# Gates and late output projections of a decoder trunk: seven products of quarters for pairs of output tiles, on half of the K tiles

## Chip, core and metric

The program runs on one core of one Trainium2 chip. The metric is the device time of one execution in microseconds, as the median of the runs shown. All matrices are float32 in DRAM.

## The reference, cut to what matters

Two layers over 512 tokens of 2048 channels; layer 0 has a state-space (SSD) mixer, layer 1 a stick-breaking attention. After each mixer comes a gate with a small embedding:

```python
h = x
for i in range(2):
    u = rms_norm(h, norm_w[i])
    mix = ssd_branch(u, ...) if i == 0 else sb_branch(u, ...)   # ends in y @ out_w, 4096 or 2048 -> 2048
    h = h + mix
    gate = sigmoid(rms_norm(h, ple_norm_w[i]) @ ple_gate_w[i])  # 2048 -> 2048
    h = h + (p[i] @ ple_proj_w[i]) * gate                       # 256 -> 2048
```

## The kernel before

Channels lie on the 128 partitions, tokens (T = 512) along the free axis; a K tile is 128 input channels. Float32 products are made from split operands: each operand is a rounded part (`ah`, `wh`, type float32r) and the difference to it (`al`, `wl`), and `mm3` makes three matmuls of 128x128 by 128x512 per K tile: wh with ah, wh with al, wl with ah. ACT makes the rounded part, DVE the difference.

`unit` (L174) makes one tile of 128 output channels: for every 8 K tiles `block` (L130) loads 512 KB of weights into `raw` (2 buffers, issued by SP), ACT copies them to `wh`, DVE subtracts to `wl` (3 buffers each), at a raised priority so that they run ahead; then 24 matmuls accumulate in one bank of PSUM. Pools `mmp` and `pxp` hold four banks each. `Flow` chains all instructions of TensorE in the order in which they are traced, whatever the scheduler does on the other engines; those run in an order that a scheduler fixes at compile time, and SP's queue of DMA issues is one of them, in order too.

The stages that the change touches, in order: the second half of K of the SSD output projection (`w_out[j][:, KT:, :]`, L551 to L555, 16 units of 16 K tiles, operands loaded back from `y_d` by `staged` through four buffers `stg`); `ple(0)` (L513), the gate, 16 units of 16 K tiles with 6 more matmuls (`px_p`) each, operands split from `h` by `norm_acts`; the attention; 8 units of 8 K tiles of its output projection (L736) beside the last head; the rest of that projection (L745): 8 units with the second 8 K tiles, 8 with all 16; and `ple(1)`. The residual `h` stays in SBUF in 16 tiles from L493 on. `act_tiles` gives 16 pairs of operand tiles that all stages share, so operands of a new stage can be split only when the last unit of the old one has read that K tile. A pool opened for a stage lies where the previous stage's pool lay, and waits tile by tile for the last reader.

## Time and profile before

| | us |
|---|---|
| median of 3 runs | 2760.46 (2760.33 to 2760.82) |
| span of the profiled execution, first to last instruction | 2757.8 |
| median less span | 2.7 |
| PE busy | 2732.7 (99%) |
| DVE busy | 1597.3 (58%) |
| ACT busy | 1188.0 (43%) |
| POOL busy | 358.4 (13%) |
| granted clock of PE, mean | 1.000 |

The span is that of one profiled execution. PE is TensorE's matmuls, PEld its weight loads, which overlap with matmuls; busy time of PE contains the latency of a matmul, so its pace is read from the distance between starts.

### The profile page before, as it was taken

Reading aid. Unit: us, or ns where it says so; the run is one execution under the profiler, and the core shown is the slowest. Engines: PE = TensorE matmul, PEld = TensorE weight load, DVE = VectorE, ACT = ScalarE, POOL = GpSimd, SP = SyncE. Lnnn points to the kernel's source line nnn. Section 1 sums busy time; section 2 is a strip of 40 time slices with the busy share of each in tenths; the row PEclk is TensorE's granted clock in tenths of the full one; section 3 lists DMA queues with packets and bytes.
Section 4 is the critical chain, followed back from the end, with each engine's and each line's share of the span. In section 5 each row is a group of like instructions: output and inputs, shape, how many; then the busy total and the mean of one; then the engine's idle time right before and its main releaser. Section 6 shows DMA issues by size and latency. Waiting matters only on the chain.

```text
span 2757.8 us, 32622 instructions
## 1 busy us (share of the span) xinstructions
PE 2732.7 (99%) x12684; PEld 2247.4 (81%) x12684; DVE 1597.3 (58%) x2226; ACT 1188.0 (43%) x1700; POOL 358.4 (13%) x363
## 2 busy tenths in 40 slices
PE   8999999999999999999999999999999999999999
PEld 6888888888888878888888888888888888888887
DVE  8676766676676774243443547647647647743533
ACT  5443444444353442232333436546646546533321
POOL 2222221212222120001101100000000000011000
PEclk9999999999999999999999999999999999999999
DMA  4342323233332446343323322322222222332332
GB/s 160 109 130 92 130 92 126 93 118 106 116 123 97 141 137 202 119 139 98 96 95 100 96 96 85 100 96 84 87 90 92 81 95 89 110 126 100 107 116 91
DMA packets 98348, 300.53 MB, mean 109 GB/s; under 512 B 10960, under 2 KB 11088, under 8 KB 98192
## 3 DMA queue, kind: packets, MB, share of 16 engines
q1 hardware_dynamic: 98192, 298.44, 33.2%
q8 instruction: 99, 1.62, 0.2%
q14 instruction: 57, 0.47, 0.1%
HBM read 280.18 MB, written 18.22 MB: 108 GB/s over the span
## 4 chain that ended last, share of the span: by engine, by line
PE 89%; DVE 5%; ACT 2%; POOL 2%; DMA 1%; issue 1%; SPq 0%; ACTq 0%; POOLq 0%; DVEq 0%
PE mm L54 74%; PE pv L54 6%; PE px_p L54 2%; DVE wl L137 1%; DVE M L410 1%; PE px_r L54 1%; PE px_z L54 1%; PE px_av L54 1%; POOL y L437 1%; PE px_st L54 1%; ACT wh L135 1%; PE px_y L54 1%; DMA stg<-y_d 1%; DVE cv L339 1%; PE px_qn L54 1%
## 5 line engine op out<-in xcount | busy, mean ns | idle before, releaser
L54 PE MATMUL mm<-ah,wh 128*128 128x512 f32 x3312 | 1300.1, 393 | 1.0 <-ACT ah L142 1.0
L54 PE MATMUL mm<-ah,wl 128*128 128x512 f32 x3312 | 1291.7, 390 | 0.0
L54 PE MATMUL mm<-al,wh 128*128 128x512 f32 x3312 | 1290.1, 390 | 1.5 <-DVE al L143 1.3
L137 DVE TENSOR_TENSOR wl<-raw,wh 128x1024 fp32r<-128x1024 f32 x457 | 569.9, 1247 | 492.3 <-ACT wh L135 491.2
L135 ACT CAST wh<-raw 128x1024 fp32r<-128x1024 f32 x457 | 478.7, 1048 | 856.7 <-PE mm L54 729.2
L54 PEld LDWEIGHTS mm<-ah,wl 128*128 128x128 f32 x3312 | 621.6, 188 | 131.9
L54 PEld LDWEIGHTS mm<-al,wh 128*128 128x128 f32 x3312 | 622.1, 188 | 130.9 <-DVE al L143 3.9
L54 PEld LDWEIGHTS mm<-ah,wh 128*128 128x128 f32 x3312 | 622.0, 188 | 126.3 <-ACT ah L142 1.2
L503 POOL TENSOR_TENSOR ssq<-ssq,sq 128x512 f32<-128x512 f32 x45 | 71.8, 1596 | 620.0 <-ACT sq L502 620.0
L410 DVE TENSOR_SCALAR M<-ab,act__370 128x128 f32<-128x128 f32 x256 | 104.8, 452 | 41.1 <-PE px_y L54 27.9
L339 DVE SCALAR_TENSOR_TENSOR cv<-xr,vec,cv 128x512 f32<-128x512 f32 x144 | 108.7, 755 | 7.0 <-ACT cv L337 4.4
L650 POOL TENSOR_SCALAR_AFFINE_SELECT lm<-lm 128x128 f32<-128x128 f32 x64 | 28.0, 438 | 615.3 <-DVE lm L649 609.6
L54 PE MATMUL pv<-wh,ah 128*128 128x512 f32 x256 | 101.0, 395 | 0.3 <-DVE gt L532 0.3
L54 PE MATMUL pv<-wl,ah 128*128 128x512 f32 x256 | 99.9, 390 | 0.0
L54 PE MATMUL pv<-wh,al 128*128 128x512 f32 x256 | 99.7, 389 | 0.0
L532 DVE TENSOR_TENSOR gt<-mm,rbc 128x512 f32<-128x512 f32 x32 | 22.1, 691 | 103.6 <-PE mm L54 103.6
L205 POOL TENSOR_TENSOR xc<-cv,sg 128x512 f32<-128x512 f32 x32 | 42.6, 1331 | 262.0 <-ACT sg L204 262.0
L203 ACT ACTIVATE sg<-cv 128x512 f32<-128x512 f32 x48 | 30.4, 633 | 104.6 <-DVE cv L339 104.3
L647 DVE SCALAR_TENSOR_TENSOR lb<-px_z,e 128x128 f32<-128x128 f32 (+1 forms) x64 | 31.4, 490 | 72.7 <-ACT e L645 72.2
L417 ACT ACTIVATE eA<-ab 64x384 f32<-64x384 f32 x64 | 33.6, 525 | 62.8 <-POOL y L437 60.3
L205 POOL TENSOR_TENSOR zs<-zs,sg 128x512 f32<-128x512 f32 x32 | 41.6, 1300 | 139.0 <-ACT sg L204 128.6
L337 ACT ACTIVATE cv<-xr,vec 128x512 f32<-128x512 f32 x48 | 39.0, 812 | 45.2 <-DVE xr L335 45.2
(219 smaller groups left out, 2557.9 us busy)
## 6 DMA issues: line engine op xcount, KB each, us to landing
raw<-in_w_in SPq DMA_DIRECT2D x160, 512.0 KB, 3.6
raw<-in_w_sb SPq DMA_DIRECT2D x96, 512.0 KB, 3.6
raw<-in_w_out SPq DMA_DIRECT2D x64, 512.0 KB, 3.9
raw<-in_w_gate SPq DMA_DIRECT2D x64, 512.0 KB, 3.5
ab<-ac_d SPq DMA_DIRECT2D x64, 256.0 KB, 3.2
raw<-in_w_v SPq DMA_DIRECT2D x32, 512.0 KB, 3.6
raw<-in_w_sbo SPq DMA_DIRECT2D x32, 512.0 KB, 3.5
y_d<-zs SPq DMA_DIRECT2D x32, 256.0 KB, 4.3
```

Of the source, the lines that this page charges most:

```text
L54: self._queue(self.tc.nc.tensor.matmul(out, lhsT, rhs, start=start, stop=stop), rows / 2370.0)
L135: S.copy(wh, raw)
L137: V.tensor_tensor(wl, raw, wh.bitcast(F32), op=ALU.subtract)
L203: S.activation(tmp, half, AF.Tanh)
L205: G.tensor_tensor(dst, half, tmp, op=ALU.mult)
L337: S.activation(cv, xr[:, 3 : T + 3], AF.Identity, bias=cb[:, u : u + 1], scale=cw[:, u, 3:4])
L339: V.scalar_tensor_tensor(cv, xr[:, tap : tap + T], cw[:, u, tap : tap + 1], cv, op0=ALU.mult, op1=ALU.add)
L410: V.tensor_scalar(M[:, c, :], ab[:, c * P : (c + 1) * P], act_[:, c, h : h + 1], act_[:, c, h : h + 1], op0=ALU.min, op1=ALU.subtract,)
L417: S.activation(eA[pp, :], ab[pp, P:], AF.Exp)
L503: G.tensor_tensor(ssq, ssq, sq, op=ALU.add)
L647: V.scalar_tensor_tensor(lb, pz, 0.0, e, op0=ALU.min, op1=ALU.subtract)
L650: G.affine_select(out=lm[:, :P], in_=lm[:, :P], compare_op=ALU.is_gt, fill=0.0, base=0, pattern=[[1, P]], channel_multiplier=-1,)
```

## The change

In the four GEMMs named above two tiles of output channels are made together by `pair`. For half of the K tiles (`SP` = 4 couples of them; in the last projection the second 8 K tiles) the product of 2x2 quarters (two output tiles by two K tiles, two halves of 256 tokens) is made with seven products in place of eight, in Winograd's form: sums and differences of weight quarters (`wforms`: S1 to S4), sums and differences of operand quarters (`xforms`, once a stage), seven accumulations of 128x128 by 128x256 into four banks Z, W, X, Y, each again by three matmuls, and a few adds of the results (`E`). The other K tiles (`rest`) follow as before, accumulated into X and Y. The first four pairs of the last projection have no rest. `EARLY`, the number of first units of the SSD projection made beside the last scan, goes from 5 to 6; `raw` becomes 8 KB a partition, and the scratch of the software DMA queue is cut to 1024 bytes. The weights are laid out in DRAM accordingly.

```diff
...
-EARLY = 5
+EARLY = 6
+SP = 4
 EARLY_SB = 8
...
-            raw = wp.tile([P, 8, P], F32, tag="raw", name="raw", bufs=2)
+            raw = wp.tile([P, 16, P], F32, tag="raw", name="raw", bufs=2)[:, :8, :]
...
+    def wforms(src):
+        with tc.high_priority(offset=4000):
+            F = wp.tile([P, 8, 2, P], F32, tag="raw", name="raw", bufs=2)
+            nc.sync.dma_start(F.rearrange("p (a b) g m -> p a b (g m)", b=2)[:, :, 0, :], src)
+            V.tensor_tensor(F[:, 1], F[:, 0], F[:, 2], op=ALU.subtract)
+            V.tensor_tensor(
+                F[:, 2:6].rearrange("p (a b) g m -> p a b (g m)", b=2)[:, :, 1, :],
+                F[:, 4].rearrange("p g m -> p (g m)").unsqueeze(1).broadcast_to([P, 2, 2 * P]),
+                F[:, 0:2].rearrange("p a g m -> p a (g m)"),
+                op=ALU.add,
+            )
+            V.tensor_tensor(F[:, 7], F[:, 6], F[:, 5], op=ALU.subtract)
+            out = []
+            for tag, a, b, pool in (("", 1, 5, wp), ("3", 5, 8, wq)):
+                wh = pool.tile([P, 2 * (b - a), P], F32R, tag="wh" + tag, name="wh")
+                wl = pool.tile([P, 2 * (b - a), P], F32R, tag="wl" + tag, name="wl")
+                raw = F[:, a:b].rearrange("p a g m -> p (a g) m")
+                S.copy(wh, raw)
+                V.tensor_tensor(wl, raw, wh.bitcast(F32), op=ALU.subtract)
+                out += [(wh, wl, 2 * i) for i in range(b - a)]
+        return out
+    def xforms(raw, i, acts):
+        for q in range(2):
+            split(*acts[2 * i + q], raw[:, 2 * q : 2 * q + 2].rearrange("p a t -> p (a t)"))
+        V.tensor_tensor(
+            raw[:, 4:6], raw[:, 0:1].broadcast_to([P, 2, H]), raw[:, 1:3], op=ALU.subtract
+        )
+        V.tensor_tensor(raw[:, 6], raw[:, 2], raw[:, 4], op=ALU.subtract)
+        V.tensor_tensor(raw[:, 7], raw[:, 3], raw[:, 6], op=ALU.subtract)
+        th = tp.tile([P, 4, H], F32R, tag=f"th{i}", name=f"th{i}")
+        tl = tp.tile([P, 4, H], F32R, tag=f"tl{i}", name=f"tl{i}")
+        split(th, tl, raw[:, 4:8])
+        return th, tl
+    def pair(src, acts, forms, k0, rest, emit, xy=None):
+        xy = xy or (mmp, "mm")
+        Z, W = (mmp.tile([P, 2, H], F32, tag="mm", name="mm") for _ in range(2))
+        X, Y = (xy[0].tile([P, 2, H], F32, tag=xy[1], name="mm") for _ in range(2))
+        begun = set()
+        def seven(bank, half, w, g, xh, xl):
+            wh, wl, i = w
+            for a, b in ((wh, xh), (wh, xl), (wl, xh)):
+                fl.mm(bank[:, half], a[:, i + g, :], b, start=bank.name not in begun, stop=False, skip_group_check=True)
+                begun.add(bank.name)
+        for b in range(len(forms) // 2):
+            S3, A11, S1, A22, S2, A12, S4 = wforms(src[:, b, :].rearrange("p (a n) -> p a n", a=4))
+            for n in range(7):
+                for g in range(2):
+                    i = 2 * b + g
+                    (ah, al), (bh, bl) = acts[k0 + 2 * i], acts[k0 + 2 * i + 1]
+                    th, tl = forms[i]
+                    lo, hi = slice(0, H), slice(H, T)
+                    seven(*(
+                        (Z, 1, A11, g, ah[:, hi], al[:, hi]),
+                        (W, 1, S3, g, th[:, 1], tl[:, 1]),
+                        (W, 0, S1, g, th[:, 0], tl[:, 0]),
+                        (Z, 0, S2, g, th[:, 2], tl[:, 2]),
+                        (X, 1, A12, g, bh[:, hi], bl[:, hi]),
+                        (X, 0, S4, g, bh[:, lo], bl[:, lo]),
+                        (Y, 1, A22, g, th[:, 3], tl[:, 3]),
+                    )[n])
+                fl.poll()
+        E = tp.tile([P, 4, H], F32, tag="E", name="E")
+        S.copy(E[:, 1], Z[:, 1])
+        U2 = tp.tile([P, H], F32, tag="U2", name="U2")
+        V.tensor_tensor(U2, Z[:, 0], E[:, 1], op=ALU.add)
+        V.tensor_tensor(E[:, 0:4:3], W, U2.unsqueeze(1).broadcast_to([P, 2, H]), op=ALU.add)
+        V.tensor_tensor(E[:, 2], W[:, 0], E[:, 3], op=ALU.add)
+        for o, ps in ((0, X), (1, Y)):
+            flat = ps.rearrange("p a t -> p (a t)")
+            for b in range(len(rest) // 8):
+                wh, wl = block(src[:, len(forms) // 2 + o + b, :].rearrange("p (k n) -> p k n", n=P))
+                for k in range(8):
+                    xh, xl = acts[rest[8 * b + k]]
+                    for a, x in ((wh, xh), (wh, xl), (wl, xh)):
+                        fl.mm(flat, a[:, k, :], x, start=False, stop=False, skip_group_check=True)
+                    fl.poll()
+            a = 2 if rest or o == 0 else 1
+            V.tensor_tensor(E[:, 2 * o + 2 - a : 2 * o + 2], ps[:, 2 - a : 2], E[:, 2 * o + 2 - a : 2 * o + 2], op=ALU.add)
+            emit(o, E[:, 2 * o : 2 * o + 2].rearrange("p a t -> p (a t)"))
...
-    def norm_acts(w):
+    def norm_acts(w, k0=0):
         acts = []
-        for k in range(KT):
+        for k in range(k0, KT):
...
+    def raw_forms():
+        return tp.tile([P, 8, H], F32, tag="U", name="U")
+    def staged_forms(src, k0, k1):
+        acts, forms = [act_tiles(k % KT) for k in range(k0, k1)], []
+        for i in range((k1 - k0) // 2):
+            U = raw_forms()
+            for q in range(2):
+                k = k0 + 2 * i + q
+                nc.sync.dma_start(U[:, 2 * q : 2 * q + 2].rearrange("p a t -> p (a t)"), src[k * P : (k + 1) * P, :])
+            forms.append(xforms(U, i, acts))
+        return acts, forms
+    def add_h(ssq=None, lq=None, j0=0):
+        def emit(o, e):
+            j = j0 + o
+            V.tensor_tensor(h[j], h[j], e, op=ALU.add)
+            if ssq is not None:
+                add_sq(lq, ssq, j)
+        return emit
     def ple(lq, layer, ssq):
-        """h += (p W) sigmoid(norm(h) Wg), by tiles of 128 channels."""
-        acts = norm_acts(plw[layer])
+        w = plw[layer]
+        acts, forms = [act_tiles(k) for k in range(2 * SP)], []
+        for i in range(SP):
+            U = raw_forms()
+            for q in range(2):
+                k = 2 * i + q
+                S.activation(
+                    U[:, 2 * q : 2 * q + 2].rearrange("p a t -> p (a t)"), h[k], AF.Copy, scale=w[:, k : k + 1]
+                )
+            forms.append(xforms(U, i, acts))
+        acts += norm_acts(w, 2 * SP)
         rbc = start_row_scale(ssq)
-        pr = lq.tile([P, 2, T], F32, tag="pr", name="pr")
-        nc.sync.dma_start(pr, pT[layer].rearrange("(k p) t -> p k t", p=P))
         ph = lq.tile([P, 2, T], F32R, tag="ph", name="ph")
         pl = lq.tile([P, 2, T], F32R, tag="pl", name="pl")
-        split(ph, pl, pr)
+        for k in range(2):
+            pr = lq.tile([P, T], F32, tag="sq2", name="pr", bufs=2)
+            nc.sync.dma_start(pr, pT[layer][k * P : (k + 1) * P, :])
+            split(ph[:, k, :], pl[:, k, :], pr)
         nssq = rp.tile([P, T], F32, tag="ssq", name="ssq")
-        for j in range(KT):
-            if j % 4 == 0:
-                vh, vl = block(w_ple[layer, j // 4])
-            psp = px("px_p")
-            for k in range(2):
-                kk = 2 * (j % 4) + k
-                mm3(psp, vh[:, kk, :], vl[:, kk, :], ph[:, k, :], pl[:, k, :], k == 0, k == 1)
-            ps = unit(w_gate[layer, j], acts)
-            gt = lq.tile([P, T], F32, tag="gt", name="gt", bufs=2)
-            V.tensor_tensor(gt, ps, rbc, op=ALU.mult)
-            S.activation(gt, gt, AF.Sigmoid)
-            V.tensor_tensor(gt, psp, gt, op=ALU.mult)
-            V.tensor_tensor(h[j], h[j], gt, op=ALU.add)
-            if layer == 0:
-                add_sq(lq, nssq, j)
-            else:
-                nc.sync.dma_start(out[j * P : (j + 1) * P, :], h[j])
+        for jj in range(KT // 2):
+            psps = []
+            for o in range(2):
+                j = 2 * jj + o
+                if j % 4 == 0:
+                    vh, vl = block(w_ple[layer, j // 4])
+                psp = px("px_p")
+                for k in range(2):
+                    kk = 2 * (j % 4) + k
+                    mm3(psp, vh[:, kk, :], vl[:, kk, :], ph[:, k, :], pl[:, k, :], k == 0, k == 1)
+                psps.append(psp)
+            def emit(o, e):
+                j = 2 * jj + o
+                V.tensor_tensor(e, e, rbc, op=ALU.mult)
+                S.activation(e, e, AF.Sigmoid)
+                V.tensor_tensor(e, psps[o], e, op=ALU.mult)
+                V.tensor_tensor(h[j], h[j], e, op=ALU.add)
+                if layer == 0:
+                    add_sq(lq, nssq, j)
+                else:
+                    nc.sync.dma_start(out[j * P : (j + 1) * P, :], h[j])
+            pair(w_gate[layer, jj], acts, forms, 0, range(2 * SP, KT), emit)
         return nssq
 
     with ExitStack() as st:
+        wq = st.enter_context(tc.tile_pool(name="wq0", bufs=2, reuse_waits="tile"))
+        tp = st.enter_context(tc.tile_pool(name="tp0", bufs=1, reuse_waits="tile"))
         lq = st.enter_context(tc.tile_pool(name="lq0", bufs=1, reuse_waits="tile"))
         for j in range(KT):
             h.append(lp.tile([P, T], F32, tag=f"h{j}", name=f"h{j}"))
             nc.sync.dma_start(h[j], (h_d if j < EARLY else xT)[j * P : (j + 1) * P, :])
         ssq = rp.tile([P, T], F32, tag="ssq", name="ssq")
         for j in range(EARLY, KT):
-            ps = unit(w_out[j][:, :KT, :], acts)
+            ps = unit(w_oe[j], acts)
             V.tensor_tensor(h[j], ps, h[j], op=ALU.add)
-        acts = staged(lq, [("stg", 4)], y_d, KT, 2 * KT)
-        for j in range(KT):
-            ps = unit(w_out[j][:, KT:, :], acts)
-            V.tensor_tensor(h[j], ps, h[j], op=ALU.add)
-            add_sq(lq, ssq, j)
+        acts, forms = staged_forms(y_d, KT, KT + 2 * SP)
+        acts += staged(lq, [("sq2", 2)], y_d, KT + 2 * SP, 2 * KT)
+        for j in range(0, KT, 2):
+            pair(w_op[j // 2], acts, forms, 0, range(2 * SP, KT), add_h(ssq, lq, j), (pxp, "px"))
         ssq = ple(lq, 0, ssq)
...
     with ExitStack() as st:
+        wq = st.enter_context(tc.tile_pool(name="wq1", bufs=2, reuse_waits="tile"))
+        tp = st.enter_context(tc.tile_pool(name="tp1", bufs=1, reuse_waits="tile"))
         lq = st.enter_context(tc.tile_pool(name="lq1", bufs=1, reuse_waits="tile"))
-        acts = half + staged(lq, [("stg", 4)], o_d, 8, KT)
+        acts, forms = staged_forms(o_d, 8, KT)
+        acts = half + acts
         ssq = rp.tile([P, T], F32, tag="ssq", name="ssq")
-        for j in range(KT):
-            early = j < EARLY_SB
-            ps = unit(w_sbo[j][:, 8:, :] if early else w_sbo[j], acts[8:] if early else acts)
-            V.tensor_tensor(h[j], ps, h[j], op=ALU.add)
-            add_sq(lq, ssq, j)
+        for j in range(0, KT, 2):
+            pair(
+                w_sp[j // 2], acts, forms, 8, () if j < EARLY_SB else range(8), add_h(ssq, lq, j), (pxp, "px")
+            )
         ple(lq, 1, ssq)
         fl.drain()
...
+def _pairs(w, strassen, rest):
+    u = _units(w, slice(None))
+    a, b = u[0::2], u[1::2]
+    blocks = []
+    for k in range(0, len(strassen), 4):
+        ka, kb = strassen[k : k + 4 : 2], strassen[k + 1 : k + 4 : 2]
+        blocks.append(np.concatenate([b[:, :, ka], a[:, :, ka], b[:, :, kb], a[:, :, kb]], axis=2))
+    for k in range(0, len(rest), 8):
+        blocks += [a[:, :, rest[k : k + 8]], b[:, :, rest[k : k + 8]]]
+    return np.ascontiguousarray(np.stack([x.reshape(x.shape[0], P, 8 * P) for x in blocks], axis=2))
...
-    nc = _bacc.Bacc("TRN2", target_bir_lowering=False, num_devices=1)
+    nc = _bacc.Bacc("TRN2", target_bir_lowering=False, num_devices=1, dynamic_dma_scratch_size=1024)
```

## Rows read from the trace of the kernel before

**Rows 1.** The page, parts 1 and 4: busy time by engine; the chain by engine.

```profile
PE 2732.7 (99%) x12684; PEld 2247.4 (81%) x12684; DVE 1597.3 (58%) x2226; ACT 1188.0 (43%) x1700; POOL 358.4 (13%) x363
...
PE 89%; DVE 5%; ACT 2%; POOL 2%; DMA 1%; issue 1%; SPq 0%; ACTq 0%; POOLq 0%; DVEq 0%
```

**Rows 2.** Windows by stage: length, busy us (count) by engine, clock, DMA.

```profile
1198.50:1374.00 175.50, 175.40 (x774) 144.74 (x773) 64.02 (x68) 56.00 (x70) 23.90 (x14) 1.00 0.35 109
1374.00:1572.00 198.00, 197.88 (x872) 163.14 (x870) 88.99 (x103) 70.95 (x90) 20.21 (x15) 1.00 0.29 96
2424.40:2467.90 43.50, 43.50 (x193) 36.04 (x192) 16.53 (x18) 13.29 (x16) 10.26 (x6) 1.00 0.30 100
2467.90:2556.00 88.10, 88.10 (x390) 72.94 (x389) 33.49 (x36) 30.53 (x39) 13.75 (x8) 1.00 0.29 96
```

**Rows 3.** Timeline of DVE, last projection: start, length, instruction.

```profile
2430.06 0.69 DVE L748 TENSOR_TENSOR h<-mm,h 128x512 f32<-128x512 f32 x1 [2.16 <-PE mm L54]
...
2435.50 0.69 DVE L748 TENSOR_TENSOR h<-mm,h 128x512 f32<-128x512 f32 x1 [3.35 <-PE mm L54]
```

**Rows 4.** Timeline of PE, a run of 256 columns in the attention.

```profile
1801.47 0.28 PE L54 MATMUL px_av<-th,vh 128*128 128x256 f32 x1
1801.59 0.28 PE L54 MATMUL px_av<-tl,vh 128*128 128x256 f32 x1
1801.70 0.28 PE L54 MATMUL px_av<-th,vl 128*128 128x256 f32 x1
```

**Rows 5.** Groups of DVE by shape: count, busy us, mean ns, idle before.

```profile
L137 DVE TENSOR_TENSOR wl<-raw,wh 128x1024 fp32r<-128x1024 f32 x457 | 569.9, 1247 | 492.3 <-ACT wh L135 491.2 <-issue 0.2
...
L143 DVE TENSOR_TENSOR al<-stg,ah 128x512 fp32r<-128x512 f32 x48 | 34.5, 749 | 5.8 <-ACT ah L142 5.5
...
L143 DVE TENSOR_TENSOR xwl<-xw,xwh 128x512 fp32r<-128x512 f32 x24 | 22.9, 954 | 20.5 <-ACT xwh L142 20.5
...
L554 DVE TENSOR_TENSOR h<-mm,h 128x512 f32<-128x512 f32 x16 | 11.1, 691 | 47.3 <-PE mm L54 47.3
...
L657 DVE TENSOR_TENSOR lm<-lm 128x256 f32<-128x256 f32 x16 | 7.2, 451 | 0.0
```

**Rows 6.** Groups of ACT by shape.

```profile
L135 ACT CAST wh<-raw 128x1024 fp32r<-128x1024 f32 x457 | 478.7, 1048 | 856.7 <-PE mm L54 729.2 <-issue 68.4 <-PE pv L54 48.5
...
L145 ACT ACTIVATE ah<-h,vec 128x512 fp32r<-128x512 f32 x48 | 31.0, 714 | 0.0
...
L142 ACT CAST ah<-stg 128x512 fp32r<-128x512 f32 x48 | 28.7, 618 | 14.5 <-DMA stg<-y_d 8.8 <-DMA stg<-o_d 5.0
```

**Rows 7.** DMA issues: count, KB each, median us to landing.

```profile
stg<-y_d SPq DMA_DIRECT2D x32, 256.0 KB, 4.1
...
stg<-o_d SPq DMA_DIRECT2D x16, 256.0 KB, 3.2
```

**Rows 8.** Timeline of DVE, last unit before the late SSD projection.

```profile
1189.69 2.49 DVE L143 TENSOR_TENSOR al<-stg,ah 128x512 fp32r<-128x512 f32 x4
```

**Rows 9.** Timeline of PE, end of the last head.

```profile
2409.22 0.39 PE L54 MATMUL px_av<-lb,v 128*128 128x128 f32 x2
```

**Rows 10.** Timeline of SP, the same place.

```profile
2410.78 1.84 SPq L160 DMA_DIRECT2D stg<-o_d  x4
```

**Rows 11.** Timeline of PE, start of the program.

```profile
13.13 0.63 PE L54 MATMUL psd<-ah,wh 128*64 128x512 f32 x1
13.56 0.63 PE L54 MATMUL psd<-al,wh 128*64 128x512 f32 x1
...
17.95 0.40 PE L54 MATMUL psd<-ah,wh 128*64 128x512 f32 x1
18.18 0.39 PE L54 MATMUL psd<-al,wh 128*64 128x512 f32 x1
```

**Rows 12.** Timeline, end of the program.

```profile
2751.92 0.69 DVE L532 TENSOR_TENSOR gt<-mm,rbc 128x512 f32<-128x512 f32 x1 [8.83 <-PE mm L54]
```

**Rows 13.** Groups of weight loads.

```profile
L54 PEld LDWEIGHTS px_av<-th,vh 128*128 128x128 f32 x48 | 9.0, 188 | 1.3
```

More of the change, by code (lines that the diff above doesn't have):

```diff
@@ L18 @@
 T = 512
+H = T // 2
 D = 2048
@@ L49, in _queue, with mm @@
         self.t += us
-    def mm(self, out, lhsT, rhs, start=True, stop=True):
+    def mm(self, out, lhsT, rhs, start=True, stop=True, **kw):
         n = int(np.prod(rhs.shape[1:]))
         rows = n if rhs.dtype == F32R else 4 * n
-        self._queue(self.tc.nc.tensor.matmul(out, lhsT, rhs, start=start, stop=stop), rows / 2370.0)
+        self._queue(self.tc.nc.tensor.matmul(out, lhsT, rhs, start=start, stop=stop, **kw), rows / 2370.0)
     def transpose(self, out, src, ident):
@@ L83, in trunk @@
 def trunk(
-    ctx: ExitStack, tc: tile.TileContext, xT, pT, vecs, hvecs, consts, w_dt, w_in, w_out, w_sb, w_v, w_sbo, w_gate, w_ple, out
+    ctx: ExitStack, tc: tile.TileContext, xT, pT, vecs, hvecs, consts, w_dt, w_in, w_oe, w_op, w_sb, w_v, w_se, w_sp, w_gate, w_ple, out
 ):
@@ L548, in trunk @@
         for j in range(EARLY, KT):
-            ps = unit(w_out[j][:, :KT, :], acts)
+            ps = unit(w_oe[j], acts)
             V.tensor_tensor(h[j], ps, h[j], op=ALU.add)
-        acts = staged(lq, [("stg", 4)], y_d, KT, 2 * KT)
-        for j in range(KT):
-            ps = unit(w_out[j][:, KT:, :], acts)
-            V.tensor_tensor(h[j], ps, h[j], op=ALU.add)
-            add_sq(lq, ssq, j)
+        acts, forms = staged_forms(y_d, KT, KT + 2 * SP)
+        acts += staged(lq, [("sq2", 2)], y_d, KT + 2 * SP, 2 * KT)
+        for j in range(0, KT, 2):
+            pair(w_op[j // 2], acts, forms, 0, range(2 * SP, KT), add_h(ssq, lq, j), (pxp, "px"))
         ssq = ple(lq, 0, ssq)
@@ L736, in trunk @@
         for j in range(EARLY_SB):
-            ps = unit(w_sbo[j][:, :8, :], half)
+            ps = unit(w_se[j], half)
             V.tensor_tensor(h[j], ps, h[j], op=ALU.add)
@@ L789, in _layout @@
         "hvecs": np.stack([i["ssd_dt_bias"][0], i["ssd_a_log"][0]], axis=1), "consts": consts,
-        "w_dt": w_dt, "w_in": _units(in_w, order), "w_out": _units(i["ssd_out_w"][0], slice(None)),
-        "w_sb": _units(i["sb_in_w"][0], sb), "w_v": wv, "w_sbo": _units(i["sb_out_w"][0], slice(None)),
-        "w_gate": np.stack([_units(i["ple_gate_w"][n], slice(None)) for n in range(2)]), "w_ple": ple,
+        "w_dt": w_dt, "w_in": _units(in_w, order), "w_oe": _units(i["ssd_out_w"][0][:D], slice(None)),
+        "w_op": _pairs(i["ssd_out_w"][0][D:], list(range(2 * SP)), list(range(2 * SP, KT))),
+        "w_sb": _units(i["sb_in_w"][0], sb), "w_v": wv, "w_se": _units(i["sb_out_w"][0][: 8 * P, : EARLY_SB * P], slice(None)),
+        "w_sp": _pairs(i["sb_out_w"][0], list(range(8, KT)), list(range(8))),
+        "w_gate": np.stack([_pairs(i["ple_gate_w"][n], list(range(2 * SP)), list(range(2 * SP, KT))) for n in range(2)]),
+        "w_ple": ple,
     }
```

## Prediction

> **What bounds the kernel now.** I read the page first: TensorE (PE) is busy for 99% of the span and the chain that ended last runs over PE for 89% [rows 1]. Then the stages that the change touches [rows 2]: in the late output projection, the first gates and both halves of the last projection PE is busy without a gap at full clock, while DVE has work for 36 to 45% and ACT for 31 to 36%. So a matmul less is a saving there, and a wait of PE is a loss at its full length. Then the price of a matmul. A unit of 8 K tiles, 24 matmuls of 512 columns, is finished every 5.44 us [rows 3]: 226.7 ns each. Matmuls of 256 columns stand only in the attention, in runs of three; there one follows the other after 0.117 us [rows 4]. Last I read the joints between the stages, because PE takes its instructions strictly in the order of `Flow`: it has nothing else to do when the operands of a new stage are late.
>
> **What is removed and added on PE.** Thirty-two pairs change (8 of w_op, 8 of w_sp, 2 x 8 gates). Each loses 2 x 8 x 3 = 48 long matmuls, 48 x 226.7 ns = 10.88 us, and gets 7 products x 4 x 3 = 84 short ones, 84 x 117 ns = 9.83 us. That is 1.05 us a pair and **33.7 us** in all. Bounds: at exactly half of the long pace (113.3 ns) it is 43.6 us, at 119 ns 28.3 us. I take 117, the row itself. The other half of K stays as it is (10.88 us a pair).
>
> **What is added on DVE and ACT in the steady state.** `wforms` replaces one `block` by three sums (256, 512, 256 elements wide) and two splits (1024 and 768). From [rows 5]: 0.45 + 0.75 + 0.45 + 1.25 + about 1.0 (between the 512 and the 1024 row) = 3.9 us of DVE instead of 1.25, twice a pair. The unfolding of Z and W takes three DVE operations (0.45 + 0.69 + 0.45), the adds of X and Y and the two adds into h four of 0.69. A late projection pair costs DVE 7.8 + 2.5 + 4.35 = 14.7 us beside 20.7 us of PE; a gate pair (five more groups: rbc, psp and half a w_ple block) 18 us beside 23.4. Both are hidden, at 71 and 77%. ACT has under 10 us a pair [rows 6]. The first four pairs of w_sp have no rest: 7.8 + 4.1 = 11.9 us of DVE against 9.83 of PE. The first of them stands behind a stall (below); the other three are short by 2.1 us each, less one set of forms made ahead (3.9): **+3 us**, bounds 0 and 8. The weights' loads arrive in four pieces a partition instead of one; they stay behind the second raw buffer: 0. `EARLY` 6 moves one unit of equal length from one side of the scan's end to the other, and PE doesn't wait there: 0. The smaller DMA scratch concerns a queue that carries nothing here: 0.
>
> **What is moved: the operands at the start of a stage.** Here I expect the loss. `xforms` needs, for each of four forms: two copies on ACT (0.62 each) and two differences on DVE (0.75 each), DVE sums of 512, 256 and 256 (0.75 + 0.45 + 0.45), the copy th of 1024 on ACT (1.05) and the difference tl on DVE (1.25) [rows 5, 6]. The shortest path from U filled to U free is 0.75 + 0.45 + 0.45 + 1.05 + 1.25 = 3.95, about 4.1 us with hand-overs; if the two differences that come first in the code run first it is 5.6. I take 5. And U has one buffer: the next two tiles can only be fetched when tl is made. A staged tile of 256 KB lands 4.1 us (y_d) or 3.2 us (o_d) after its issue [rows 7], the second issue is about 0.5 us later: 4.5 us. So a form comes every **9.5 us** (bounds 8 and 10.5), and the first pair's second block waits for forms 2 and 3 at once: its fourth product (of 42 matmuls, nine are before it) needs form 3, and 33 x 0.117 = 3.9 us follow.
>
> - w_op. In the last unit before it, the act tiles come free one by one and the splits of tiles 0 to 3 run at 1189.69 [rows 8]; the second is done at 1191.0, and U's second filling can be issued. Three cycles later, 1191.0 + 28.5 = 1219.5, form 3 is there; the first pair's Strassen part ends at 1223.4 instead of 1198.5 + 9.8 = 1208.3: **+15 us** (10.5 to 18).
> - w_sp. tp1 lies where the attention's tiles were, and U, behind 12 KB of wq1, comes to lie over vl and v3. Their last reader is the last head's product at 2409.22 [rows 9]; the kernel before issues its own staged loads there at 2410.78 [rows 10]. U filled 2414.3, form 0 at 2419.3, form 3 at 2447.8, end of the part 2451.7 instead of 2424.4 + 9.8 = 2434.2: **+17.5 us** (11.8 to 21).
> - Second gates. U is filled by ACT (two of 0.714 [rows 6]), so a cycle is 1.4 + 5 = 6.4 us. But forms write act tiles 0 to 7, which the last pair of w_sp reads as its rest, in Y's pass last: tiles 0 and 1 are free 4.1 us before the pair's end, U 2.7 before it. Form 3 is there 16.6 after the end, the part ends at 20.5 instead of 2.7 (px_p) + 9.8 = 12.5: **+8 us** (5 to 12.5).
> - First gates. Here the forms' act tiles were Strassen operands and are free 15 us before the end: the chain is in time. But DVE has 31 us of work (forms 16, weights 9, evictions and p's split 6) in the 24.5 us until form 3 is needed, some of it movable: **+4 us** (0 to 10).
>
> **Clock.** In the first stage matmuls of 512 columns come 0.43 us apart at 13.13 and 0.23 apart at 17.95 [rows 11]: the lower and the upper of the two levels, ten matmuls at 0.2 us too much. After the two long stalls I expect as much, 2 x 2 = **+4 us** (0 to 6).
>
> **Tail.** Between the last matmul and the output stands one more DVE add, 0.69, ahead of the one at 2751.92 [rows 12]: **+0.7 us**.
>
> Sum: -33.7 + 15 + 17.5 + 8 + 4 + 3 + 4 + 0.7 = +18.5 us. The span of 2757.8 becomes 2776.3; with the 2.7 us that lie between it and the median of 2760.46 it is **2779 us**, 0.7% slower.
>
> **Rivals.**
> (1) The forms come in time and it is faster. At w_sp this hangs on one thing, the place of U: o_d's tiles of heads 8 to 13 are stored long before, and if U is over tiles that are free early, only form 3 waits for the last head's store; the stall and its clock go, 2779 - 19.5 = 2759.5. From there each microsecond off the cycle takes 6 us away (w_op and second gates), and from 0.7 us on it is faster by over 0.2%; with all low ends 2745, and without any of the four stalls 2779 - 44.5 - 4 = 2730. For it: before, the splits follow the freed tiles closely [rows 8]. Against it: 4.1 + 1.05 + 1.25 us of landing, th and tl are rows and cannot shrink. Chance 0.30.
> (2) DVE becomes the bound. The difference xwl takes 954 ns where 749 stand for one of the same shape [rows 5]; were DVE's new work longer by a quarter, the four bare pairs would need 14.9 us against 9.83, +15 us beyond the sum, the gate pairs 22 of 23.4: 2794 to 2805. Against it: these stages show no such long rows. Chance 0.08.
> (3) The seven products save nothing. Each matmul has its own weight load of 188 ns [rows 13]. If loads could not overlap, 84 x 188 ns = 15.8 us a pair instead of 9.83: 2779 + 191 = 2970; at 129.5 ns a short matmul costs what the long ones did, 2813. Against it: in [rows 4] three follow at 0.117 although each load has that length. Chance 0.04.
> The Trainium skill, page "TensorE: Matmul & The Clock Gate", Part 3 (Packing small matmuls, what overlaps and what doesn't), says that a weight load overlaps matmuls in flight only where the row groups differ; all groups are used here, and its section on LDWEIGHTS gives 107 ns for 128 columns. By that a pair would take 84 x (117 + 107) against 48 x (227 + 107) ns, 2.8 us more, about 89 us over the 32. The trace doesn't agree: 226.7 ns for 512 columns leave no room for 107 more.
>
> **How the numbers follow.** About 0.2% (5.5 us) is what a measurement of this kernel can tell from no change. My sum: chance 0.58, with a range of its own of 2762 to 2803, of which 0.04 fall within 0.2%. Rival 1: 0.30, of which 0.22 faster and 0.08 within 0.2%. Rivals 2 and 3: 0.12, slower. Faster 0.22, same 0.12, slower 0.66. All low ends together give 2745, all high ends 2808; the range of 8 in 10 leaves out the ends where several of them fall together: 2748 to 2803.
>
> **What would show it.** PE's matmuls of 256 columns 0.115 to 0.119 us apart in the middle of a pair; a pair of w_op finished every 20.7 us, a gate pair every 23.4. PE waiting for DVE tl or al in the first pair of w_op and of w_sp, 10 us and more in one piece, after the sixth or seventh group of the second block; refills of U 8 to 10 us apart in SP's queue, none before 2410 at w_sp; a shorter wait at the second gates. It is wrong if the refills come closer together, if U at w_sp is filled before the last head ends, or if short matmuls stand further apart than 0.119 over a whole pair.

## The result and the profile after

The changed kernel takes 2831.5 us (2830.61 to 2832.64) beside 2760.39 of the kernel before on the same chip: ratio 1.0255, 95% interval 1.024 to 1.0269, some 71 us slower. The direction was forecast; the size (2779, range to 2803) was not. The span grew by 73.1 us, from 2757.8 to 2830.9. First the page, its engine line and the chain by engine, to hold against [rows 1].

```profile
PE 2731.9 (97%) x13836; PEld 2297.4 (81%) x13836; DVE 1878.9 (66%) x2708; ACT 1273.5 (45%) x1830; POOL 356.0 (13%) x363
...
PE 81%; DVE 10%; DMA 3%; ACT 3%; POOL 1%; issue 1%; SPq 0%; ACTq 0%; DVEq 0%; POOLq 0%
```

PE's idle time (span less busy) grew from 25 to 99 us, and the chain moved from PE (89 to 81%) to DVE (5 to 10), ACT (2 to 3) and DMA (1 to 3). PE's busy time fell by less than 1 us, since a matmul behind a wait or at the lower clock has a longer record. So the 73 us are waits, and the slow stretches behind them. The windows by stage say where; they answer to [rows 2] (w_op with the 2 us before it; first gates; the last 15 us before w_sp, with the end of the last head, and the first pair of w_sp; the rest of w_sp; second gates; columns as there).

```profile
1197.80:1389.90 192.10, 174.90 (x1059) 158.28 (x1058) 128.28 (x184) 75.27 (x98) 18.45 (x13) 0.94 0.34 102
1389.90:1605.00 215.10, 194.23 (x1147) 170.81 (x1146) 156.42 (x212) 88.61 (x120) 24.78 (x15) 0.96 0.29 89
2448.60:2500.00 51.40, 31.60 (x150) 26.85 (x149) 32.23 (x50) 15.82 (x21) 0.00 (x0) 0.77 0.28 87
2500.00:2614.40 114.40, 114.40 (x785) 106.89 (x784) 96.05 (x136) 50.43 (x68) 20.43 (x13) 1.00 0.34 102
2614.40:2830.90 216.50, 194.94 (x1156) 173.65 (x1154) 148.34 (x212) 75.50 (x97) 3.26 (x2) 0.96 0.33 103
```

Every stage that begins with forms has PE idle and a granted clock under 1; the stretch from 2500 to 2614.4, three bare pairs and four full ones, has neither. Next the pace of the short matmuls, PE's timeline in a pair of w_sp that waits for nothing:

```profile
2535.04 0.28 PE L56 MATMUL mm<-th,wh 128*128 128x256 f32 x1
2535.16 0.29 PE L56 MATMUL mm<-tl,wh 128*128 128x256 f32 x1
```

They stand 0.120 us apart, not 0.117, and that is also their mean over the seven pairs from 2500 to 2614.4. With that, and with 226.7 ns for a long one, each gap between two starts on PE has a nominal length. The gaps' excess over it, added up stage by stage, is called the loss below (it holds waits and slow clock alike). The sum for the changed kernel:

| | forecast | measured |
|---|---|---|
| 32 pairs: 48 x 226.7 against 84 matmuls | -33.7 | -25.6 (84 x 120.0) |
| start of w_op, with its clock | +15 + 2 | +24.0 |
| start of the first gates | +4 | +19.6 |
| later pairs of the first gates | 0 | +7.5 |
| start of w_sp, with its clock and the bare pairs | +17.5 + 2 + 3 | +26.8 |
| start of the second gates | +8 | +19.6 |
| tail | +0.7 | +0.7 |
| sum | +18.5 | +72.6 |

**Start of w_op.** PE's waits between 1198 and 1235 (waited for: total, times, longest), then SP's DMA issues there:

```profile
PE mm L56 <- ACT ah L144: 10.8, 1, 10.8
PE mm L56 <- ACT th L144: 4.2, 2, 2.6
PE mm L56 <- DVE tl L145: 2.1, 2, 1.4
```

```profile
1194.62 0.81 SPq L617 DMA_DIRECT2D U<-y_d  x2
...
1205.37 0.80 SPq L617 DMA_DIRECT2D U<-y_d  x2
...
1218.66 0.80 SPq L617 DMA_DIRECT2D U<-y_d  x2
```

The first of these three comes 3.6 us after the 1191.0 of the forecast: U still held tiles whose splits could not be made before an act tile came free, and DVE made the second of them last:

```profile
1193.91 0.69 DVE L145 TENSOR_TENSOR al<-U,ah 128x512 fp32r<-128x512 f32 x1
```

The next two follow 10.75 and 13.3 us apart where 9.5 was forecast. ACT's timeline over the third form shows what was left out of that cycle:

```profile
1209.32 0.62 ACT L144 CAST ah<-U 128x512 fp32r<-128x512 f32 x1 [4.41 <-DMA U<-y_d]
1211.18 0.83 ACT L210 CAST wh<-raw 128x768 fp32r<-128x768 f32 x1 [1.24 <-PE mm L56]
1212.12 1.05 ACT L137 CAST wh<-raw 128x1024 fp32r<-128x1024 f32 x1
1213.07 0.61 ACT L144 CAST ah<-U 128x512 fp32r<-128x512 f32 x1
...
1216.34 1.04 ACT L144 CAST th<-U 128x1024 fp32r<-128x1024 f32 x1 [1.61 <-DVE U L223]
```

Between the two copies of one form stand two copies of weights, the first of them waiting until PE frees a weight buffer: 3.1 us for a row of 0.6. The forecast put the steps of a form end to end and gave ACT and DVE to it alone. After the wait PE runs at the lower of its two clock levels (granted clock 0.50 from 1223 to 1231.7):

```profile
1223.27 0.58 PE L56 MATMUL mm<-ah,wh 128*128 128x256 f32 x1 [10.76 <-ACT ah L144]
...
1229.99 0.42 PE L56 MATMUL mm<-th,wl 128*128 128x256 f32 x1
1230.21 0.42 PE L56 MATMUL mm<-th,wh 128*128 128x256 f32 x1
...
1232.07 0.28 PE L56 MATMUL mm<-ah,wh 128*128 128x256 f32 x1
1232.19 0.28 PE L56 MATMUL mm<-al,wh 128*128 128x256 f32 x1
```

Starts 0.21 us apart turn into 0.12 at 1231.9. The lower level was there ahead of the long wait too: from 1205.8 to 1211.3, behind waits of 2.6 and 1.4 us, PE is busy without a gap and the granted clock is 0.50. In the whole trace some 90 short matmuls stand 0.213 apart, 90 x 0.093 = 8 us; with the long ones 0.43 apart behind the gates' waits (below) it is about 11, forecast 4.

**Start of the first gates.** PE's waits from 1385 to 1420, SP's issue of p with the one before it, and POOL's last add of w_op:

```profile
PE px_p L56 <- ACT ph L144: 9.2, 1, 9.2
PE px_p L56 <- DVE pl L145: 7.1, 1, 7.1
```

```profile
1395.87 0.34 SPq L135 DMA_DIRECT2D raw<-in_w_gate  x1
1396.26 2.87 SPq L647 DMA_DIRECT2D pr<-in_pT  x2
```

```profile
1397.31 1.46 POOL L597 TENSOR_TENSOR ssq<-ssq,sq 128x512 f32<-128x512 f32 x1 [4.01 <-ACT sq L596]
```

The stage's first products are the small ones of p. Before, p had a tile of its own and was fetched some 270 us ahead of its use:

```profile
1103.13 0.43 SPq L518 DMA_DIRECT2D pr<-in_pT  x1
```

Now `pr` lies in the two buffers of `sq2`, which the squares of w_op's last pairs hold: its second half is issued at 1398.80, right after POOL's add. Its first half goes out with the weight load ahead of it in SP's queue, which had to wait for a raw buffer until DVE's difference ended at 1395.84. Then the splits of p stand among the forms on DVE. PE was waiting for that from 1391.8 to 1409, and its clock came back only four us later:

```profile
1409.49 0.63 PE L56 MATMUL px_p<-ph,wl 128*128 128x512 f32 x1
1409.92 0.63 PE L56 MATMUL px_p<-ph,wh 128*128 128x512 f32 x1
...
1412.90 0.39 PE L56 MATMUL px_p<-pl,wh 128*128 128x512 f32 x1
1413.13 0.39 PE L56 MATMUL px_p<-ph,wl 128*128 128x512 f32 x1
```

At the second gates it is the same: 12.3 us for ph.

### The profile page after: what moved, and what is told of

It reads as the page before. It is cut to its first block, busy times and chain, and to the rows that moved or that the text cites. A ratio compares the mean times of both kernels' runs of the same rounds, so it can differ in the third digit from the quotient of the medians.

```text
span 2830.9 us, 35583 instructions
## 1 busy us (share of the span) xinstructions
PE 2731.9 (97%) x13836; PEld 2297.4 (81%) x13836; DVE 1878.9 (66%) x2708; ACT 1273.5 (45%) x1830; POOL 356.0 (13%) x363
## 4 chain that ended last, share of the span: by engine, by line
PE 81%; DVE 10%; DMA 3%; ACT 3%; POOL 1%; issue 1%; SPq 0%; ACTq 0%; DVEq 0%; POOLq 0%
PE mm L56 66%; PE pv L56 6%; DVE wl L139 2%; DMA raw<-in_w_gate 2%; PE px_p L56 1%; DVE M L504 1%; PE px_r L56 1%; PE px_z L56 1%; DVE al L145 1%; PE px_av L56 1%; ACT wh L137 1%; DVE wl L211 1%; POOL y L531 1%; DMA raw<-in_w_sp 1%; PE px_st L56 1%
## 5 line engine op out<-in xcount | busy, mean ns | idle before, releaser
L56 PE MATMUL mm<-ah,wh 128*128 128x512 f32 (+1 forms) x3184 | 1213.3, 381 | 26.5 <-ACT ah L144 25.7
L56 PE MATMUL mm<-ah,wl 128*128 128x512 f32 (+1 forms) x3184 | 1204.2, 378 | 3.7 <-DVE wl L139 3.7
L56 PE MATMUL mm<-al,wh 128*128 128x512 f32 (+1 forms) x3184 | 1202.6, 378 | 2.0 <-DVE al L145 1.6
L210 ACT CAST wh<-raw 128x768 fp32r<-128x768 f32 (+1 forms) x128 | 115.7, 940 | 166.2 <-DVE raw L204 131.2
L211 DVE TENSOR_TENSOR wl<-raw,wh 128x768 fp32r<-128x768 f32 (+1 forms) x128 | 141.9, 1112 | 25.4 <-ACT wh L210 24.4
L56 PE MATMUL mm<-th,wh 128*128 128x256 f32 x512 | 149.6, 292 | 8.5 <-ACT th L144 8.5
L56 PE MATMUL mm<-tl,wh 128*128 128x256 f32 x512 | 149.7, 292 | 4.6 <-DVE tl L145 4.6
L56 PE MATMUL mm<-th,wl 128*128 128x256 f32 x512 | 148.6, 290 | 0.0
L56 PEld LDWEIGHTS mm<-th,wh 128*128 128x128 f32 x512 | 101.7, 199 | 10.2 <-ACT th L144 9.8
L56 PEld LDWEIGHTS mm<-tl,wh 128*128 128x128 f32 x512 | 101.9, 199 | 5.9 <-DVE tl L145 5.9
L56 PEld LDWEIGHTS mm<-th,wl 128*128 128x128 f32 x512 | 102.1, 199 | 0.0
```

The costliest lines, as they stand in the source:

```text
L56: self._queue(self.tc.nc.tensor.matmul(out, lhsT, rhs, start=start, stop=stop, **kw), rows / 2370.0)
L210: S.copy(wh, raw)
L211: V.tensor_tensor(wl, raw, wh.bitcast(F32), op=ALU.subtract)
```

## Experiments

Each kernel was timed in several rounds beside the kernel before, whose median moved between 2760.39 and 2761.47 from one group of rounds to the next; a difference of 1 or 2 us between two changed kernels shows nothing. The diff is against the changed kernel where no other is named, and shortened.

**halves: the price of a short matmul by itself.** In the kernel before, every matmul of the late SSD units is issued as two halves.

```
+ for c in range(2):
+     cs = slice(256 * c, 256 * c + 256)
+     fl.mm(ps[:, cs], a[:, k, :], x[:, cs], ...)
```

> The kernel before, with nothing of the change but the short matmuls: in the 16 units of the late SSD projection each of the 768 matmuls of 512 columns is made as two of 256, on the same weights. Theory A, a matmul costs its columns and 32 cycles more (120.0 ns against 226.7): 768 x 13.3 ns = +10.2 us over before. Theory B, my forecast's price of 117 ns: +5.6 us. Theory C, half of the long pace: 0.

Measured 2771.01 against 2760.99, ratio 1.0036 (1.0023 to 1.0048): +10.0 us. DVE's evictions show a unit of 96 halves every 11.52 us, 120.0 ns each, with no form, no wait and full clock:

```profile
1303.80 0.69 DVE L561 TENSOR_TENSOR h<-mm,h 128x512 f32<-128x512 f32 x1 [3.65 <-PE mm L54]
1315.32 0.69 DVE L561 TENSOR_TENSOR h<-mm,h 128x512 f32<-128x512 f32 x1 [3.65 <-PE mm L54]
```

That is theory A; the 5.6 us of theory B lie below the interval (6.3 to 13.3 us). So 25.6 us is all that the change can win. The 117 was no misreading of the attention: all 88 gaps between short matmuls there lie between 0.112 and 0.119 us, 0.117 in the mean. But they stand in runs of two or three, and a stream of short matmuls goes at 0.120.

**own_p: p ahead of the forms.** In the changed kernel p is fetched through U and split before the gates' forms.

```
+ U = raw_forms()
+ for k in range(2):
+     pr = U[:, 2 * k : 2 * k + 2]
+     nc.sync.dma_start(pr, pT[layer][...]); split(ph[:, k, :], pl[:, k, :], pr)
  for i in range(SP): U = raw_forms() ...
```

> The changed kernel with one edit: the two tiles of p are loaded into U ahead of the gate's forms, not into the buffers sq2, which the sums of squares hold until the last residual tile. Theory P (the gates start late because p comes late): the waits of px_p, 17 us at the first gates and 15 at the second, go; what is left is the chain of forms, 6 to 10 us at each, so 15 to 25 us less than the changed kernel: 2807 to 2817. Theory F (the chain of forms is the bound anyway, as in my forecast): at most 6 us less.

Measured 2829.42, ratio 1.0248 (1.0234 to 1.0262): 2 us of the 39, no more than the noise and by the time theory F. The waits for ph and pl are gone, and others stand in their place; PE's waits from 1385 to 1420:

```profile
PE mm L56 <- ACT ah L144: 4.6, 1, 4.6
PE mm L56 <- DVE tl L145: 2.0, 1, 2.0
PE mm L56 <- ACT th L144: 1.6, 1, 1.6
PE px_n L56 <- POOL ssq L597: 1.5, 1, 1.5
```

The loss at the first gates goes from 19.6 to 14.3, at the second it grows to 23.0, of which waits for ah, th, al and tl are 15.3. The late p was what PE waited for, but the forms were no earlier: ACT fills U for the last two at 1393.40 and 1405.94, before the edit at 1392.67 and 1404.47.

**ring: U in two buffers.** Raw tiles in two buffers of [P, 4, H], the sums in a tile of their own; to make room, `U2` lies in `E` and a small tile of the attention in another pool.

```
- U = tp.tile([P, 8, H], F32, tag="U")
+ U = tp.tile([P, 4, H], F32, tag="U", bufs=2)
+ sums = tp.tile([P, 4, H], F32, tag="US")      # in xforms
```

> The changed kernel with the staged tiles in two buffers of their own and the sums in a third, so that the next load need not wait for tl. Theory U (one buffer sets the distance of the forms): the second block of the first pair comes 8 to 12 us earlier in the late SSD projection and in the last projection, and 15 to 25 us go in all: 2807 to 2817. Theory W (the forms come late because DVE and ACT make weights first): under 6 us go.

Measured 2813.27, ratio 1.0188 (1.0175 to 1.0202): 18 us back, theory U. Four tiles are now fetched at once:

```profile
1195.87 2.92 SPq L618 DMA_DIRECT2D U<-y_d  x4
```

w_op loses 12.6 instead of 24.0, w_sp 18.4 instead of 26.8. The single buffer was thus half of the one and a third of the other. What is left still hangs on U: at w_op these fillings wait for the splits of the two forms before them (`al`, 1195.15 to 1195.84 and 1197.23 to 1197.91), and at w_sp the third form's tiles are issued at 2455.16, 14.2 us after the first's.

**no_pool: first gates without POOL's adds.** `add_sq` in the first gates computes the squares but leaves out their 15 additions to the sum, so the norm behind it is wrong.

```
- G.tensor_tensor(ssq, ssq, sq, op=ALU.add)
+ if add: G.tensor_tensor(ssq, ssq, sq, op=ALU.add)
```

> The changed kernel without the adds of the sums of squares on POOL during the first gates (15 adds left out; the norm of the attention's input then holds one tile's square only). Theory G (POOL's adds hold DVE up, and so the weights, in the pairs of the first gates that take 25 to 27 us instead of 23.7): these pairs run at 23.7 and about 8 us go: 2823. Theory H (the two raw buffers and their loads set it): no change, 2831.

Measured 2825.75, ratio 1.0232 (1.0218 to 1.0246): -5.7 us, theory G with about 6 of its 8; the loss in the later gate pairs falls from 7.5 to 2.0. What it was, in the changed kernel's timelines of POOL and DVE:

```profile
1514.93 2.01 POOL L597 TENSOR_TENSOR ssq<-ssq,sq 128x512 f32<-128x512 f32 x1 [18.26 <-ACT sq L596]
```

```profile
1514.58 1.22 DVE L211 TENSOR_TENSOR wl<-raw,wh 128x1024 fp32r<-128x1024 f32 x1
1515.71 1.78 DVE L664 TENSOR_TENSOR E<-E,rbc 128x512 f32<-128x512 f32 x1
```

and the same operation without the add, 0.68 us, and an add that no instruction of DVE meets, 1.29:

```profile
1512.64 0.68 DVE L665 TENSOR_TENSOR E<-E,rbc 128x512 f32<-128x512 f32 x1
```

```profile
1268.53 1.29 POOL L597 TENSOR_TENSOR ssq<-ssq,sq 128x512 f32<-128x512 f32 x1 [3.06 <-ACT sq L596]
```

DVE's operation ends 0.55 us after POOL's add does, so it did next to nothing in the 1.2 us beside it. The add was held up in its turn: it began beside DVE's difference of 1.22 us, which took no longer for it. The Trainium skill, page "SBUF — State Buffer", section "SBUF: two separate sides", says that DVE and GpSimd share a port pair as an exclusive lock, which a DVE operation with two operands in SBUF needs too when GpSimd's reads SBUF, and that the one that starts second blocks entirely. The trace agrees, with 1.78 us for 0.68 and 2.01 for 1.29.

**own_p_ring: both.** The first four lines of own_p on top of ring.

> Both edits, p through U and two buffers for the staged tiles. Theory P (late p and the one buffer of U are two causes in series): px_p waits no longer and the forms are 8 us earlier, so the gates' starts lose 4 to 8 us each in place of 20, and the whole is 30 to 40 us under the changed kernel: 2792 to 2800. Theory F (DVE has too much to do at the start of a gate, whatever is loaded when): the gates' starts still lose 13 us and more each, and the whole stays over 2803.

Measured 2799.76, ratio 1.0137 (1.0122 to 1.0152): -32 us, more than 2 + 18. With p early, the second buffer pays at the gates too: 10.6 and 15.6 lost. That is the time of theory P, at its edge, but the starts lose more than the 4 to 8 us that it allowed.

**gates_rest: the other half of K first.** On top of it, the first pair of each gate does the long matmuls of the rest, which need no forms, before the seven products.

```
+ if first:
+     others(0, X); others(1, Y)
```

> As the kernel with both edits, and in the first pair of each gate the 96 long matmuls of the rest run ahead of the Strassen part, 10.9 x 2 = 21.8 us on PE in which the forms can be made. If the forms are what is late (both theories), the gates' starts lose 0 to 4 us each: 2775 to 2788. If the operands of the rest are late as well (their splits stand behind the forms on DVE), no gain over both edits: 2792 and more.

Measured 2794.24, ratio 1.0117 (1.01 to 1.0134), the second case; the interval overlaps that of own_p_ring. The gates' starts lose 9.2 and 10.4; the first now waits 6.6 us for `al` of the rest, whose splits were traced behind the forms. The cover is also half of what was expected: in the trace 48 long matmuls stand ahead of the first pair's short ones, 10.9 us, not 96 and 21.8.

**best: the same for w_op and w_sp.** Rest first at w_op with its tiles staged in more buffers; w_sp's pairs in the order 8, 0, 10, 2, ..., full and bare in turn; second gates with seven products on h[8] to h[15].

```
- for j in range(0, KT, 2):
+ for j in (8, 0, 10, 2, 12, 4, 14, 6):
```

> As that, and the same at the late SSD projection (rest first, its eight operands staged through six buffers into the act tiles that come free first) and at the last projection (pairs with rest and without by turns, the first of them with rest and rest first; the second gates take the other half of K for the sums, which is ready first). Work on PE is that of the changed kernel. If the starts of the stages are all that was lost, what is left is 25.6 us of shorter matmuls less about 7 us of DVE against POOL in the first gates and a few us elsewhere: 2740 to 2752, under the kernel before. If DVE is the bound of the stages as well, 2765 and more.

Measured 2789.1, ratio 1.0102 (1.0087 to 1.0117): the four starts still lose 48 us, and by the time it is the second case, though the waits below are not shown to be DVE's load. w_sp falls to 10.7, w_op only to 10.2, and the second gates rise to 18.0, some 12 of them one wait of px_n for POOL's sum of squares. PE at w_op still waits for the same link, although 10.9 us of rest now stand ahead of it:

```profile
1223.14 0.58 PE L56 MATMUL mm<-th,wh 128*128 128x256 f32 x1 [5.39 <-ACT th L144]
```

**forms_ahead: the order alone.** The changed kernel with the forms ahead of the weights in the scheduler's order.

```
  def xforms(raw, i, acts):
+     with tc.high_priority(offset=8000):
```

> The changed kernel with the forms of the operands at a higher priority than the weights on ACT and DVE. Theory W (a form takes 11 to 13 us in place of my 9.5 because weights stand ahead of it in the in-order queues): refills of U 9 to 10 us apart, 4 to 6 us less lost at the late SSD projection and at the last projection each, 2815 to 2823. Theory U (the chain of one form is that long by itself): refills still 11 us and more apart, 2828 and more.

Measured 2830.6, ratio 1.0254 (1.0239 to 1.027): nothing. At w_op the loss is 21.1 instead of 24.0, at w_sp 26.6 as before. SP's refills, and DVE between the second landing (1210.0) and the third refill:

```profile
1205.98 0.80 SPq L618 DMA_DIRECT2D U<-y_d  x2
1217.61 0.80 SPq L618 DMA_DIRECT2D U<-y_d  x2
```

```profile
1211.88 0.95 DVE L211 TENSOR_TENSOR wl<-raw,wh 128x768 fp32r<-128x768 f32 x1
...
1213.69 1.22 DVE L139 TENSOR_TENSOR wl<-raw,wh 128x1024 fp32r<-128x1024 f32 x1
```

The edit did not do what it was made for: two differences of weights still stand inside the form, 2.2 us of this cycle of 11.63; 9.5 is what remains without them. So the rows account for the cycle, but the time of this run speaks neither for nor against it.

**apart: sums apart from the operands.** On top of best: U feeds the sums only; the tiles that are also operands are fetched a second time into other buffers and split there, rest first; the norm's factor of the gates is due later.

```
- for q in range(2): split(*acts[2 * i + q], raw[...])    # in xforms
+ forms = staged_forms(y_d, KT, KT + 2 * SP)
+ other = staged(lq, tags, y_d, KT + 2 * SP, 2 * KT, 8)
+ acts = staged(lq, tags, y_d, KT, KT + 2 * SP, 8) + other
```

> As the kernel that takes the rest first everywhere, and the sums of operands apart from the operands: the staged tiles are loaded a second time for the sums alone, so that the forms wait for no act tile; in the gates the splits of the rest stand ahead of the forms; the norm's factor of the gates is asked for later (18 in place of 5 us of products), since its matmul waited 11.8 us for POOL's last add. Theory S (the order at the starts is what is left): 54 us of loss at the five places fall to 20 to 30, 2755 to 2766. Theory D (DVE's sum of work at the starts is the bound, in whatever order): 45 us and more stay, 2780 and more.

Measured 2782.51 against 2761.47, ratio 1.0074 (1.0061 to 1.0086), by the time theory D. But w_op loses nothing, which theory D had not foreseen. Its forms are no faster, they are early: U feeds no act tile any more, so its last filling does not wait for the units before, and the last form is made 60 us ahead of the stage. SP's issue and DVE's last step (in best these stand at 1206.02 and 1223.12):

```profile
1124.27 0.79 SPq L628 DMA_DIRECT2D U<-y_d  x2
```

```profile
1135.95 1.23 DVE L145 TENSOR_TENSOR tl<-US,th 128x1024 fp32r<-128x1024 f32 x1 [1.12 <-ACT th L144]
```

First gates 6.6, w_sp 9.1. The second gates lose 27.3.

**apart_dve: squares of the first gates added on DVE.**

```
- G.tensor_tensor(ssq, ssq, sq, op=ALU.add)
+ eng.tensor_tensor(ssq, ssq, sq, op=ALU.add)      # V in the first gates
```

> The same, and the 15 adds of the sums of squares of the first gates on DVE in place of POOL. Theory G (POOL's adds hold DVE up longer than DVE would need for them itself): 3 to 6 us less than the same without. If DVE is merely full there, no change or some us more.

Measured 2779.52, ratio 1.0063 (1.0049 to 1.0077). Its intervals overlap those of apart; the loss in the gate pairs falls from 4.5 to 1.9. Windows by stage (w_op, first gates, w_sp, second gates):

```profile
1197.30:1373.00 175.70, 175.70 (x1092) 159.22 (x1092) 129.93 (x187) 81.41 (x109) 19.51 (x14) 1.00 0.37 110
1373.00:1566.80 193.80, 188.44 (x1136) 166.68 (x1135) 150.17 (x219) 82.95 (x109) 1.29 (x1) 1.00 0.33 96
2421.30:2556.00 134.70, 126.71 (x862) 118.63 (x861) 108.71 (x160) 61.93 (x85) 17.11 (x12) 0.97 0.34 104
2556.00:2772.40 216.40, 198.42 (x1156) 175.87 (x1155) 153.97 (x220) 75.56 (x95) 4.85 (x3) 0.94 0.33 101
```

The last head's products end 3.5 us ahead of the kernel before (2405.8 against 2409.3), the last matmul 20.9 behind it (2772.4 against 2751.5). Layer 1 alone is what makes this version slower: 12.8 us of gain against 11.1 lost at w_sp and 26.6 at the second gates.

**layer0 and op_only: only where it pays.** layer0 has apart_dve's first layer and the second layer of the kernel before; op_only has seven products in w_op alone.

```
- acts, forms = staged_forms(o_d, 8, KT); pair(w_sp[j // 2], ...); ple(lq, 1, ssq)
+ ps = unit(w_sbo[j][:, 8:, :] if early else w_sbo[j], ...); ple_units(lq, 1, ssq)
- ssq = ple(lq, 0, ssq)                             # op_only
+ ssq = ple_units(lq, 0, ssq, ...)
```

> As apart_dve up to the attention (seven products in the late SSD projection and in the first gates), and everything behind the attention as in the kernel before: single units of 24 or 48 long matmuls, no forms, squares on POOL. If the gain of a pair is 0.80 us (84 at 120 ns against 48 at 226.7) and the losses stay where the trace of apart_dve has them, 16 pairs give 12.8 us, the start of the first gates takes 6.6 and the gate pairs about 1 to 2: the last head ends about 3.5 us ahead of the kernel before, and nothing behind it changes, so 2757 us, ratio 0.9987 (0.9975 to 0.9995). The rival, that what a stage gains is lost again at the next joint: the last projection or the second gates wait longer, and the time is that of the kernel before, ratio 0.9995 to 1.001.

> Seven products in the eight pairs of the late SSD projection alone, with the start of apart (rest first, forms' sums loaded apart, two buffers); first gates, last projection and second gates as single units as before. By 0.80 us a pair it gains 6.4 us; the start of this projection lost nothing in apart, and the first gates need no forms: 2754 to 2756 us, ratio 0.998 (0.9973 to 0.999), the best that the change has to give at one stage. The rival, that the joint eats the gain: the splits for the first gates come out of other tiles and beside the unfolding of the last pair, PE waits there for 3 us or more, ratio 0.999 to 1.001.

Both 2755.88 against 2760.62: layer0 ratio 0.9981 (0.9972 to 0.9989), op_only 0.9985 (0.9976 to 0.9994). Both beat the kernel before, by some 4 to 5 us, and can't be told from each other; op_only does it with under a quarter of the new DVE work (66 us more than before against 282 in the changed kernel). Its window of w_op:

```profile
1197.50:1370.00 172.50, 172.50 (x1079) 156.56 (x1078) 123.52 (x175) 71.99 (x95) 20.03 (x14) 1.00 0.36 107
```

w_op has no gap, and the gates begin 7.2 us earlier than before (first product of p 1365.7 against 1372.9), of which the seven products account for 6.4; 2.0 us are lost there again, 1.3 of them where px_n waits for POOL's squares.

## Why the prediction was too low

- **The price of the short matmul (-33.7).** Mis-sized: 120.0 ns, outside the bound of 119 that the text gave, so 0.80 us a pair and 25.6 in all. 8 of the 54 us that were missed. Shown by halves. 117 is the attention's pace; what failed was to carry it from runs of three over to a stream.
- **Start of w_op (+15) and of w_sp (+17.5, +3, and +4 of clock).** The mechanism was right: one buffer U, refills after tl, PE waiting in the first pair's second block (10.8 us in one piece at w_op and 9.8 at w_sp, though for `ah`, after that block's first product). The cycle of 9.5 us was mis-sized: 10.8 and 13.3 at w_op, where the first refill was 3.6 us late as well; 15.3, 8.9 and 12.5 at w_sp (issues at 2450.04, 2465.38, 2474.27 and 2486.75). 7.0 and 4.3 us; at w_sp it would be 7.3, had the +3 for the bare pairs not been too much. ring shows the buffer's share, 11 and 8 us; best against apart (10.2 and 0 lost at w_op) what holds the rest there: a filling of U that is also split into act tiles waits for the stage before, and with it the forms that need only U. How much of the cycle the weights between a form's steps make up is read from rows alone; forms_ahead, meant to try it, left them there.
- **First gates (+4, "the chain is in time").** The step that failed most, 15.6 us. The text counted DVE's work and said nothing of where p's tile lies: the diff moves `pr` from its own tile into `sq2`, and so its DMA from 270 us ahead of its use to 5 us behind the joint. own_p shows that this was the wait in front, and that the forms' chain, held to be in time, costs 14 us right behind it: U is filled for the last three forms at 1377.86, 1392.67 and 1404.47, 14.8 and 11.8 us apart.
- **Second gates (+8).** The same two causes by the waits, 11.6 us more: 12.3 us for ph in the changed kernel, and 15.3 us for the operands and forms in own_p, where p is early.
- **Gate pairs (0, "hidden at 77%").** 7.5 us. DVE's load was not far off (a window share of 73% over the first gates), but POOL's adds hold up the DVE instruction that meets them, 0.69 us becoming 1.78 or 1.22 becoming 1.54, and the weights come late. Shown by no_pool.
- **Bare pairs (+3), tail, EARLY, scratch.** The bare pairs cost nothing: after 2500 w_sp has no loss. The tail is right, and no run sets the two zeros against anything else.
- **Rivals.** The first (forms in time) falls for the changed kernel; at w_sp the refill came at 2450.04, behind the last head's product as forecast. Yet op_only is this rival made true at w_op, once nothing but U holds the forms. The second (DVE the bound) came true in a part only: no row of DVE got longer but those beside POOL. The third falls: weight loads of 189 to 192 ns in the mean (changed kernel, halves) stay hidden at 120 ns a matmul, against the rule of the Trainium skill cited there. The same section names another case in which a load is pulled ahead, that of the background weight buffer; no run here tells whether this is it.

What stays open is the second gates in apart and apart_dve. PE waits there for `ah` of the rest (7.0 us) and `th` (4.9), and POOL's last squares end only at 2577.7; which of the two orders, the splits' or the squares', holds the other up was not tried, nor whether DVE simply has too much to do there. Nor was a version of w_sp with the early units' work moved behind its first pair.

## What to carry to other kernels

A change that makes the products that it touches 7% shorter (0.80 of 10.88 us) has to be costed at its joints first: here 25.6 us of steady gain stood against the starts of four stages, and where the operands of a new stage passed through one buffer and two engines, PE lost 19 to 27 us each time. Give what such a stage stages a buffer of its own, and keep what can be made early free of tiles that the stage before still reads: that took w_op's loss from 10.2 to 0. Work ahead that needs no new operands helped by less than its length: with 10.9 us of it the gates' starts still lost 9.2 and 10.4. Check for every tile that a diff renames which loads thereby move behind other readers. A price on which the sum hangs is to be taken from a stream like the one that the change makes: runs of two and three stood at 0.117 us, the stream at 0.120.
